# Sample states of the retention heads: values from float32 weights on four column groups, and their scores summed in the bank of the state products

## The chip, the cores and the metric

The kernel runs on one core of one Trainium2 chip. A core has five engines that run side by side and wait for each other by semaphores: PE (matrix products; the trace shows its weight loads apart, as PEld), DVE (vectors), ACT (activations and copies), POOL (general vector work, no access to the PE's accumulators) and SP, which here only issues transfers. Products go into PSUM, eight banks of 128 partitions x 512 float32. The metric is the device time of the whole kernel in microseconds (us). The kernel before takes 2159.27 us, the median of three runs (2158.21 to 2162.92); lower is better.

## The reference

The program is one inference step of one layer: 1024 prompt tokens, and 32 sample tokens (8 sequences of 4 tokens, each with its own past). Two branches read the same normalised input: retention (4 heads, keys of 256, values of 512) and latent attention. The change touches the retention of the sample tokens alone, which the reference computes with one chunk of four tokens for each sequence:

```python
def retention_chunk(q, k, v, s_prev, log_g):
    ...
    scores = jnp.einsum('bihd,bjhd->bhij', q, k) * dmask[None]
    intra = jnp.einsum('bhij,bjhe->bihe', scores, v)
    q_decay = jnp.exp((idx[:, None] + 1.0) * log_g[None, :])
    cross = jnp.einsum('bihd,bhde->bihe', q, s_prev) * q_decay[None, :, :, None]
    k_decay = jnp.exp((c - 1.0 - idx)[:, None] * log_g[None, :])
    s_new = (jnp.exp(c * log_g)[None, :, None, None] * s_prev
             + jnp.einsum('bjhd,bjhe->bhde', k * k_decay[None, :, :, None], v))
    return intra + cross, s_new
```

`q`, `k`, `v` are columns of `rmsnorm(x) @ w_in`, q and k turned by position. `intra + cross` is then group-normalised over each head's 512 values, scaled and multiplied by a SiLU gate. The states `s_prev` and `s_new` (8 x 4 x 256 x 512 float32, 16.8 MB each) are inputs and outputs of the kernel.

## The kernel before

**Stages.** The normalised input is kept turned (features on partitions, the 1056 = 1024 + 32 tokens along the free side) as eight pairs `xn[k]` of a rounded high part and the rest, in the fast float32 format (fp32r). A product of full accuracy is three fast ones, `mac` (L265 to L267): high by high, low by high, high by low. Stages follow each other: latents, page attention of the sample tokens, retention (the stage of the change, about 727 to 1340 us of the trace), latent attention of the prompt, and the output projections.

**A retention head.** `head_qk` (filler for the head before it) makes q and k of all tokens, 128 columns at a time, and leaves those of the sample tokens in `qS` and `kS`. `head_w` fetches the head's value weights, eight tiles of 128x512, and splits each into `X["W"][k]`, high and low. `prompt_chunks` then walks the eight prompt chunks. `values_of` makes a chunk's values in tiles tagged `vnh` and `vnl` (two buffers each). Behind the chunks comes `sample_state`.

**sample_state of before.** The sample tokens' values are made in eight steps of two fast products (L1006): the stationary side is `few`, 64 columns, the 32 sample columns of the high and the low input side by side; the moving side is the high and then the low split weight, 512 columns. Rows 0 to 31 and 32 to 63 of the result, copied out as `vs` (L1009), still have to be added; each later product that reads `vs` does so, because its other operand is repeated for both halves. L1012 makes the scores of the sample tokens, masked into `sm` (64x32). L1017 (`turn`) spreads the values to 128 rows, for row group r (32 rows) the tokens of sequences 2r and 2r + 1 in four copies, from which the update of the states takes a split of keys and values.

Then come four turns, one for each pair (i, m) of sequence parity and key half. A turn multiplies the queries with the states of four sequences at once (L1038): four products with a 128x32 stationary side, each on its own group of 32 columns of the array and so on its own 32 rows of the one bank `px`. Four products (L1045) make the update, DVE adds it to the states (L1047), and two transfers store them (L1049); the states of the turn after next come into the buffers that this frees (`states`, L978).

After the last turn the bank is copied out (L1054) as `xs`, and two float32 products close the head: the scores by the values (L1056), and `sel` by `xs` (L1057), which picks each token's row out of the four row groups. `group_norm` works on the 32 rows, and `gate_out` turns them with four transposes (L865) and multiplies them with the gate. For heads 0 to 2 `gate_out` is put off (`late`) into the next head's first chunk.

**What sets the order.** The functions are Python generators. A `yield` gives a cost, and `woven` lets that stream go on which is furthest behind, as a share of its declared total: the rest of a head's chunks and `sample_state` (27.9; 32.4 in the last head) against the next head's q, k and weights (50.3), in the last head against the remaining gate projections (31.8). What is woven in from there is the filler below. The order that the generators give is the priority for a planner, which sets each engine's order of instructions and the waits when the program is built, by its own model of times; a tile's slot is given on when the last reader of the old tile is done. On the chip each engine goes through its list in that order. All transfers here are issued by SP, so one that waits holds those behind it.

The last head differs: before the filler runs, five tiles of latents and two of rotary keys for the next stage are asked for (L1083, L1086), into the slots of the split value weights.

Of the kernel before, what the change touches and what calls it, by code (L numbers as in the profile page):

```python
# [9 lines left out]
F32 = mybir.dt.float32  # L10
F32R = mybir.dt.float32r
# [3 lines left out]
ALU = mybir.AluOpType  # L15
# [4 lines left out]
P = 128  # L20
D = 1024
SEQ = 1024
NB = 8
NS = 4
# [37 lines left out]
def _constants():  # L62
# [4 lines left out]
    def put(name, val, rows=P):  # L67
        o, w = at[name]
        c[:rows, o:o + w] = val
# [10 lines left out]
                                         for g in lg], 1), (4, 1)))  # L80
    put("sel", (p[:, None] % NR) == r[None, :])
    copy, token = p % 32 // 8, p // 32 * 8 + p % 8
# [8 lines left out]
    put("kd", np.exp((P - 1.0 - p[:, None]) * lg[None]) / 16)  # L91
    put("qdS", np.exp((rt[:, None] + 1.0) * lg[None]), NR)
    put("qd2S", np.exp(2 * (rt[:, None] + 1.0) * lg[None]), NR)
    put("kdS", (copy < 3)[:, None] * np.exp((NS - 1.0 - p[:, None] % NS) * lg[None]) / 16)
# [67 lines left out]
def decode_step(ctx: ExitStack, tc: tile.TileContext, A: dict, O: dict):  # L162
# [20 lines left out]
    def ac():  # L183
        return banks["pool"].tile([P, 512], F32, tag="ac", name="ac", bufs=3)
# [7 lines left out]
    def b32(ap):  # L192
        return ap.bitcast(F32)
# [576 lines left out]
    p4 = ph.enter_context(tc.tile_pool(name="p4", bufs=1))  # L770
    turn = p4.tile([2 * NR, P], F32, name="turn")
    sp.dma_start(turn, A["consts"][:2 * NR, at["turn"][0]:])
# [89 lines left out]
    def gate_out(h, on, n, cols, g):  # L862
        pt = tr()
        for f in range(4):
            pe.transpose(pt[:, f * P:f * P + n], on[:n, f * P:(f + 1) * P], ident[:n, :n])  # L865
# [116 lines left out]
    def sample_state(h, X):  # L982

        q, k = X["qS"], X["kS"]
        g4 = float(np.exp(NS * lg[h]))
        sl = slice(SEQ, NT)
        ks = p4.tile([P, 2, 4, 4, 8], F32, tag="knh", name="ks", bufs=2)
        for m in range(2):
# [5 lines left out]
        act.activation(kt, pt[:, :DK], AF.Copy, scale=C("kdS", h, 1))  # L994
        ks = p4.tile([P, 2, 2, NR], F32, tag="knh", name="ks2", bufs=2)
        for m in range(2):
            pool.tensor_copy(ks[:, m], k[:, m].unsqueeze(1).to_broadcast([P, 2, NR]))
        qm = p4.tile([P, 2, 288], F32, tag="row", name="qm", bufs=2)
        pool.memset(qm, 0.0)
        for m in range(2):  # L1000
            pool.tensor_copy(qm[:, m].rearrange("p (b x) -> p b x", x=36)[:, :, :NS], q[:, m].rearrange("p (b t) -> p b t", t=NS))
        yield 1.0
        ps = ac()
        for n in range(8):
            for part in range(2):
                pe.matmul(ps[:2 * NR], few[:, n, :], X["W"][n][part], start=n + part == 0, stop=n == 7 and part == 1)  # L1006
            yield 0.45
        vs = p4.tile([2 * NR, DV], F32, tag="vnl", name="vs", bufs=2)
        act.copy(vs, ps[:2 * NR])  # L1009
# [18 lines left out]
        yield 1.0  # L1028
        px = ac()
        g = gate_in(h, NR, sl)  # L1030
        out = O["ret_sample"][0].rearrange("(r i) h (m p) e -> i m h p r e", i=2, m=2)
        turns = [(i, m) for i in range(2) for m in range(2)]
        loaded = X["st"]
        for n, (i, m) in enumerate(turns):
            pairs = loaded.pop(0)
            st = [pairs[r // 2][:, r % 2, :] for r in range(4)]
            for r in range(4):
                ins = pe.matmul(px[32 * r:32 * r + 32, :], qm[:, m, 32 * (2 * r + i):32 * (2 * r + i) + 32], st[r],  # L1038
                                start=n == 0, stop=n == 3, tile_position=(0, 32 * r), skip_group_check=True)
                if n > 1:  # L1040
                    tc.keep_in_program_order(ins)
# [14 lines left out]
        pe.matmul(po[:NR], sm, vs, start=True, stop=False)  # L1056
        pe.matmul(po[:NR], C("sel"), xs, start=False, stop=True)  # L1057
# [558 lines left out]
```

## Time and profile before

| What | before |
|---|---|
| median of three runs | 2159.27 us |
| the profiled execution | 2150.59 us |
| span of its trace | 2148.7 us |
| PE busy | 2107.3 us, 98% |
| DVE, ACT, POOL busy | 1261.0, 723.7, 326.4 us |
| value steps L1006, all heads | 64 products, 18.6 us busy |
| state products L1038, all heads | 128 records, 18.9 us busy |
| granted PE clock, mean | 0.996 |

The profile is one execution. Each row of the trace is one instruction with its start from the beginning of the span and its length; equal ones in a row are merged with their count. An instruction's place is given by its line in the kernel (L1006), its result and operands by the names of tiles (`ac<-wv,few`: into a bank of tag ac, from `wv` and `few`), its form by the stationary side (128*64) and the moving side. Matmuls overlap: the next starts before the one before has ended, so lengths don't add up, but starts do. A float32 product shows as two records. A row of the list of waits reads: who waited, for whom, the sum, how many times, the longest.

### The profile page before, as it was taken

To read this page: it belongs to the slowest core of one execution; us is meant where nothing else is said; L and a number is where in the kernel's file an instruction comes from. 1 tells how busy PE (TensorE), PEld (TensorE's weight loads), DVE (VectorE), ACT (ScalarE), POOL (GpSimd) and SP (SyncE) were. 2 spreads that over 40 slices of the span, in tenths; PEclk is the share of its full clock that TensorE was granted. 3 is DMA by queue.
4 is the path that set the end of the run, shared out by engine and by line. 5 is a ranking of instruction groups with operands and counts; after the bars stand their busy time and mean duration, and the time that the engine had idled before them with its cause. 6 is when DMAs were issued, how large, how long until landed. Compare 5 with 4: busy or idle time off the path is not lost.

```text
span 2148.7 us, 38490 instructions
## 1 busy us (share of the span) xinstructions
PE 2107.3 (98%) x15192; PEld 1841.5 (86%) x15192; DVE 1261.0 (59%) x2832; ACT 723.7 (34%) x1514; POOL 326.4 (15%) x519
## 2 busy tenths in 40 slices
PE   8999999999999999999999999999999999999998
PEld 7898787777777998888888887788888999999998
DVE  5534556565565357676676764877776353444465
ACT  5412222342433322222222312454555341322343
POOL 2210111111110022222222220122211000000122
PEclk9999999999999999999999999999999999999999
DMA  7476656566564422644634637210112453324243
GB/s 209 124 221 232 233 194 234 212 231 237 200 231 165 124 65 72 206 115 121 197 75 147 179 87 259 58 45 18 38 51 80 151 176 95 100 80 127 79 144 118
DMA packets 325876, 307.83 MB, mean 143 GB/s; under 512 B 91648, under 2 KB 283264, under 8 KB 321600
## 3 DMA queue, kind: packets, MB, share of 16 engines
q1 hardware_dynamic: 316480, 221.50, 34.6%
q0 software_dynamic: 9216, 83.89, 10.5%
q8 instruction: 119, 1.95, 0.4%
q14 instruction: 61, 0.50, 0.1%
HBM read 236.96 MB, written 68.36 MB: 142 GB/s over the span
## 4 chain that ended last, share of the span: by engine, by line
PE 87%; DVE 2%; ACT 1%; DMA 1%; issue 1%; POOL 1%; SPq 0%; ACTq 0%; DVEq 0%; POOLq 0%
PE mm L265 22%; PE mm L266 20%; PE mm L267 20%; PE sc L655 4%; PE x L686 3%; PE ac L267 2%; PE ac L265 2%; PE ac L266 2%; PE mm L1313 2%; PE tr L1299 1%; PE tr L865 1%; PE ac L1038 1%; PE ac L1256 1%; PE x L680 1%; PE ac L887 1%
## 5 line engine op out<-in xcount | busy, mean ns | idle before, releaser
L265 PE MATMUL mm<-xh,wh 128*128 128x352 f32 x1344 | 455.2, 339 | 0.2
L267 PE MATMUL mm<-xh,wl 128*128 128x352 f32 x1344 | 434.3, 324 | 2.1 <-DVE wl L199 2.1
L266 PE MATMUL mm<-xl,wh 128*128 128x352 f32 x1344 | 434.9, 324 | 0.0
L265 PEld LDWEIGHTS mm<-xh,wh 128*128 128x128 f32 x1344 | 252.2, 188 | 90.5 <-issue 76.5
L266 PEld LDWEIGHTS mm<-xl,wh 128*128 128x128 f32 x1344 | 253.3, 188 | 3.3 <-issue 1.0
L267 PEld LDWEIGHTS mm<-xh,wl 128*128 128x128 f32 x1344 | 253.0, 188 | 3.3 <-DVE wl L199 2.6
L199 DVE TENSOR_TENSOR wl<-wr,wh 128x512 fp32r<-128x512 f32 (+2 forms) x251 | 173.8, 704 | 120.4 <-ACT wh L246 101.8
L246 ACT CAST wh<-wr 128x512 fp32r<-128x512 f32 x216 | 129.8, 618 | 294.9 <-PE mm L266 221.0
L651 DVE STREAM_TRANSPOSE kt<-craw 128x512 f32<-128x512 f32 x256 | 160.7, 681 | 84.8 <-PE sc L655 79.7
L416 ACT ACTIVATE gev<-mm 128x352 f32<-128x352 f32 x120 | 55.6, 464 | 237.2 <-PE mm L267 157.0
L267 PE MATMUL mm<-gh,wl 128*128 128x352 f32 x384 | 124.3, 324 | 0.0
L267 PE MATMUL mm<-mh,wl 128*128 128x352 f32 x384 | 124.3, 324 | 0.0
L265 PE MATMUL mm<-mh,wh 128*128 128x352 f32 x384 | 124.3, 324 | 0.0
L265 PE MATMUL mm<-gh,wh 128*128 128x352 f32 x384 | 124.3, 324 | 0.0
L266 PE MATMUL mm<-ml,wh 128*128 128x352 f32 x384 | 124.2, 324 | 0.0
L266 PE MATMUL mm<-gl,wh 128*128 128x352 f32 x384 | 124.2, 323 | 0.0
L265 PE MATMUL mm<-wv,xh 128*128 128x512 f32 x256 | 103.7, 405 | 0.0
L266 PE MATMUL mm<-wv,xh 128*128 128x512 f32 x256 | 100.9, 394 | 0.0
L267 PE MATMUL mm<-wv,xl 128*128 128x512 f32 x256 | 100.7, 394 | 0.0
L655 PE MATMUL sc<-kt,q 32*32 32x512 f32 x2560 | 91.2, 600 | 0.0
L854 ACT ACTIVATE on<-ac,gb,gs 128x512 f32<-128x512 f32 (+1 forms) x36 | 28.0, 778 | 179.6 <-DVE gb L852 179.6
L1546 POOL TENSOR_TENSOR xr<-x1h,x1l 128x352 f32<-128x352 f32 x24 | 27.1, 1154 | 389.9 <-DVE pT L199 311.9
(382 smaller groups left out, 4540.0 us busy)
## 6 DMA issues: line engine op xcount, KB each, us to landing
wr<-in_w_in_dram SPq DMA_DIRECT2D x144, 256.0 KB, 3.1
st<-in_state_ret_dram SPq DMA_DIRECT2D x32, 512.0 KB, 4.5
out_ret_sample_dram<-st SPq DMA_DIRECT2D x32, 512.0 KB, 3.8
wr<-in_w_ple_gate_dram SPq DMA_DIRECT2D x48, 256.0 KB, 2.9
gt<-gev SPq DMA_DIRECT2D x48, 176.0 KB, 3.9
gl<-go SPq DMA_DIRECT2D x16, 528.0 KB, 5.8
gate<-ga SPq DMA_DIRECT2D x16, 528.0 KB, 3.5
g<-gt SPq DMA_DIRECT2D x32, 256.0 KB, 3.2
```

The source lines that it names most:

```text
L199: dve.tensor_tensor(out=out, in0=src, in1=b32(hi), op=ALU.subtract)
L246: hi_by[0](hi, raw)
L265: pe.matmul(out, wh, xh, start=first, stop=False)
L266: pe.matmul(out, wh, xl, start=False, stop=False)
L267: pe.matmul(out, wl, xh, start=False, stop=last)
L416: act.activation(t, ps, func)
L651: dve.transpose(kt[:, 2 * i + s].rearrange("p (n r) -> p n r", r=32), src)
L655: pe.matmul(sc[32 * v:32 * v + 32, q, :], Q["q4"][qs_, j + v // 2, 2 * (g % 2) + v % 2, :], kt[qs_, v, :], start=n == 0, stop=n == NJ // 2 ...
L686: pe.matmul(pv[32 * v:32 * v + 32, :KL], pT[:, n, 32 * v:32 * v + 32], keys[v % 2][:, 8 * (v // 2) + n, :], start=n == 0, stop=n == 7, til ...
L854: act.activation(on[:n], po, AF.Identity, bias=nb[:n], scale=s[:n])
L1313: pe.matmul(po[:, :256], v[a][w], t[:, x, 256 * a:256 * a + 256], start=j + a + part == 0, stop=False, skip_group_check=True)
L1546: pool.tensor_tensor(out=xr, in0=b32(x1[f][0][:, sl]), in1=b32(x1[f][1][:, sl]), op=ALU.add)
```

## The change

- The values of the sample tokens come from the plain float32 weights, read from memory once more: eight tiles `wvS` of 128x512 (256 KB) a head, in the slots of `vnh` and `vnl`. Four are asked for at the start of `sample_state`, each of the other four after the value step whose slot it takes.
- The stationary side is `xS`, the sum of the high and low input (128x32, float32). A step is four float32 products, one for each 128 of the 512 columns and each on its own group of 32 columns of the array, into 32 rows and 128 columns of the bank.
- Four copies put these blocks on the diagonal of `vs`, now 128x512, made once, with zeros elsewhere. `turn` has 128 rows and adds the row groups.
- The scores are made for 128 rows and masked into `sm`, 128x128, with zeros outside the eight rows of each group. Their product with `vs` opens the bank `px`, and the state products add to it.
- The copy of the bank and the two closing products are gone. `group_norm` works on the 128 rows of the bank, and `gate_out` turns and picks the rows in one, by float32 products with `sel` (four of 128x128 by 128x32) in place of the transposes.
- Yields: 2.5 instead of 1.0 ahead of the values; 0.24 instead of 0.45 for a value step, 1.0 for the fourth; 0.3 instead of 1.0 at the end.

The constants `sel`, `qdS` and `qd2S` follow the new rows. The rest of the diff:

```diff
-    few = p4.tile([P, 8, 2 * NR], F32R, name="few")
+    xS = p4.tile([P, 8, NR], F32, name="xS")
     for k in range(8):
-        for part in range(2):
-            pool.tensor_copy(few[:, k, part * NR:(part + 1) * NR], b32(xn[k][part][:, SEQ:]))
+        pool.tensor_tensor(out=xS[:, k], in0=b32(xn[k][0][:, SEQ:]), in1=b32(xn[k][1][:, SEQ:]), op=ALU.add)
+    vs = p4.tile([P, DV], F32, name="vs")
+    pool.memset(vs, 0.0)
...
-            pe.transpose(pt[:, f * P:f * P + n], on[:n, f * P:(f + 1) * P], ident[:n, :n])
+            o = pt[:, f * P:f * P + n]
+            if n == P:
+                pe.transpose(o, on[:, f * P:(f + 1) * P], ident)
+            else:
+                pe.matmul(o, on[:, f * P:(f + 1) * P], C("sel"), start=True, stop=True)
...
+        def weights(k):
+            raw = p4.tile([P, DV], F32, tag="vn" + "hl"[k % 2], name="wvS", bufs=2)
+            sp.dma_start(raw, w_in[k * P:(k + 1) * P, C_RV + h * DV:C_RV + (h + 1) * DV])
+            return raw
+
+        raws_ = [weights(k) for k in range(4)]
...
-        yield 1.0
+        yield 2.5
         ps = ac()
         for n in range(8):
-            for part in range(2):
-                pe.matmul(ps[:2 * NR], few[:, n, :], X["W"][n][part], start=n + part == 0, stop=n == 7 and part == 1)
-            yield 0.45
-        vs = p4.tile([2 * NR, DV], F32, tag="vnl", name="vs", bufs=2)
-        act.copy(vs, ps[:2 * NR])
+            for r in range(4):
+                pe.matmul(ps[r * NR:(r + 1) * NR, :P], xS[:, n], raws_[n][:, r * P:(r + 1) * P], start=n == 0, stop=n == 7,
+                          tile_position=(0, r * NR), skip_group_check=True)
+            if n < 4:
+                raws_.append(weights(n + 4))
+            yield 1.0 if n == 3 else 0.24
+        for r in range(4):
+            rs = slice(r * NR, (r + 1) * NR)
+            act.copy(vs[rs, r * P:(r + 1) * P], ps[rs, :P])
         pss = tr()
         for m in range(2):
-            pe.matmul(pss[:2 * NR, :NR], ks[:, m].rearrange("p c x -> p (c x)"), q[:, m], start=m == 0, stop=m == 1)
-        sm = p4.tile([2 * NR, NR], F32, tag="sms", name="sms", bufs=1)
-        dve.tensor_tensor(out=sm, in0=pss[:2 * NR, :NR], in1=C("maskS", h, NR, 2 * NR), op=ALU.mult)
+            pe.matmul(pss[:, :NR], ks[:, m].rearrange("p c x -> p (c x)"), q[:, m], start=m == 0, stop=m == 1)
+        sm = p4.tile([P, 4, NR], F32, tag="smr", name="sms", bufs=1)
+        pool.memset(sm, 0.0)
+        dve.tensor_tensor(out=sm[:, :, :8], in0=pss[:, :NR].rearrange("p (r x) -> p r x", x=8),
+                          in1=C("maskS", h, NR).rearrange("p (r x) -> p r x", x=8), op=ALU.mult)
...
         px = ac()
+        pe.matmul(px, sm.rearrange("p r x -> p (r x)"), vs, start=True, stop=False, skip_group_check=True)
...
-                                start=n == 0, stop=n == 3, tile_position=(0, 32 * r), skip_group_check=True)
+                ins = pe.matmul(px[32 * r:32 * r + 32, :], qm[:, m, r, i], st[r], start=False, stop=n == 3,
+                                tile_position=(0, 32 * r), skip_group_check=True)
...
-        xs = p4.tile([P, DV], F32, tag="row", name="xsb", bufs=2)
-        act.copy(xs, px)
-        po = ac()
-        pe.matmul(po[:NR], sm, vs, start=True, stop=False)
-        pe.matmul(po[:NR], C("sel"), xs, start=False, stop=True)
-        on = group_norm(po[:NR], NR, C("qdS", h, 1, NR), C("qd2S", h, 1, NR))
-        yield 1.0
+        on = group_norm(px, P, C("qdS", h, 1), C("qd2S", h, 1))
+        yield 0.3
```

More of the change, by code (lines that the diff above doesn't have):

```diff
@@ L80, in _constants @@
                                          for g in lg], 1), (4, 1)))
-    put("sel", (p[:, None] % NR) == r[None, :])
+    put("sel", (p[:, None] // 32 * 8 + p[:, None] % 32 == r[None, :]) & (p[:, None] % 32 < 8))
     copy, token = p % 32 // 8, p // 32 * 8 + p % 8
@@ L91, in _constants @@
     put("kd", np.exp((P - 1.0 - p[:, None]) * lg[None]) / 16)
-    put("qdS", np.exp((rt[:, None] + 1.0) * lg[None]), NR)
-    put("qd2S", np.exp(2 * (rt[:, None] + 1.0) * lg[None]), NR)
+    put("qdS", np.exp((t[:, None] + 1.0) * lg[None]))
+    put("qd2S", np.exp(2 * (t[:, None] + 1.0) * lg[None]))
     put("kdS", (copy < 3)[:, None] * np.exp((NS - 1.0 - p[:, None] % NS) * lg[None]) / 16)
@@ L770, in decode_step @@
     p4 = ph.enter_context(tc.tile_pool(name="p4", bufs=1))
-    turn = p4.tile([2 * NR, P], F32, name="turn")
-    sp.dma_start(turn, A["consts"][:2 * NR, at["turn"][0]:])
-    few = p4.tile([P, 8, 2 * NR], F32R, name="few")
+    turn = p4.tile([P, P], F32, name="turn")
+    sp.dma_start(turn, A["consts"][:, at["turn"][0]:])
+    xS = p4.tile([P, 8, NR], F32, name="xS")
     for k in range(8):
-        for part in range(2):
-            pool.tensor_copy(few[:, k, part * NR:(part + 1) * NR], b32(xn[k][part][:, SEQ:]))
+        pool.tensor_tensor(out=xS[:, k], in0=b32(xn[k][0][:, SEQ:]), in1=b32(xn[k][1][:, SEQ:]), op=ALU.add)
+    vs = p4.tile([P, DV], F32, name="vs")
+    pool.memset(vs, 0.0)
     tok = slots(p4, "tok", 4)
@@ L994, in sample_state @@
         act.activation(kt, pt[:, :DK], AF.Copy, scale=C("kdS", h, 1))
-        ks = p4.tile([P, 2, 2, NR], F32, tag="knh", name="ks2", bufs=2)
+        ks = p4.tile([P, 2, 4, NR], F32, tag="knh", name="ks2", bufs=2)
         for m in range(2):
-            pool.tensor_copy(ks[:, m], k[:, m].unsqueeze(1).to_broadcast([P, 2, NR]))
-        qm = p4.tile([P, 2, 288], F32, tag="row", name="qm", bufs=2)
+            pool.tensor_copy(ks[:, m], k[:, m].unsqueeze(1).to_broadcast([P, 4, NR]))
+        qm = p4.tile([P, 2, 4, 2, 32], F32, tag="row", name="qm", bufs=2)
@@ L999, in sample_state @@
         pool.memset(qm, 0.0)
         for m in range(2):
-            pool.tensor_copy(qm[:, m].rearrange("p (b x) -> p b x", x=36)[:, :, :NS], q[:, m].rearrange("p (b t) -> p b t", t=NS))
-        yield 1.0
+            for i in range(2):
+                pool.tensor_copy(qm[:, m, :, i, NS * i:NS * i + NS], q[:, m].rearrange("p (r i t) -> p r i t", i=2, t=NS)[:, :, i])
+        yield 2.5
         ps = ac()
         for n in range(8):
-            for part in range(2):
-                pe.matmul(ps[:2 * NR], few[:, n, :], X["W"][n][part], start=n + part == 0, stop=n == 7 and part == 1)
-            yield 0.45
```

1 line of the change is left out of this document (removed).

## The prediction

> **What bounds the kernel now.** I read the page's busy shares first, then who made the PE wait in the retention stage that the change touches (860 to 1345 us), then the PE's instructions in order of time there, and last the DMA share and the queue around the last head.
>
> ```profile
> PE 2107.3 (98%) x15192; PEld 1841.5 (86%) x15192; DVE 1261.0 (59%) x2832; ACT 723.7 (34%) x1514; POOL 326.4 (15%) x519
> ...
> PE ac L265 <- POOL wqr L196: 1.7, 1, 1.7
> PE ac L267 <- DVE ll L199: 0.9, 1, 0.9
> PE ac L1038 <- DMA st<-in_state_ret_dram: 0.5, 1, 0.5
> ```
>
> The last three rows are the PE's longest waits in those 485 us, 3.1 us together, each of them once, and all in or behind the last head; the first two belong to the next stage. The reader sees that the sample states of the first three heads run with the PE never idle to speak of: there a PE microsecond saved is one saved, and work of ACT, DVE, POOL or DMA costs nothing until the PE waits for it. So the sum is one of PE time, made against the profiled execution (2150.59 us) and then carried to the median of 2159.27 us by the same difference; the 8.7 us between these two aren't explained by anything here.
>
> **The old pieces, priced.** Head 0, the PE's starts in order of time (start, length, instruction):
>
> ```profile
> 874.20 0.63 PE L1006 MATMUL ac<-wv,few 128*64 128x512 f32 x2
> 874.67 0.32 PE L265 MATMUL mm<-xh,wh 128*128 128x352 f32 x1
> ...
> 879.45 2.01 PE L1006 MATMUL ac<-wv,few 128*64 128x512 f32 x8
> ...
> 884.67 1.12 PE L1017 MATMUL tr<-vs,turn 64*128 64x512 f32 x2
> 885.72 0.43 PE L265 MATMUL mm<-xh,wh 128*128 128x352 f32 x1
> ...
> 889.31 1.06 PE L1038 MATMUL ac<-st,qm 128*32 128x512 f32 x8
> 890.30 0.50 PE L1045 MATMUL ac<-vst,kx 32*128 32x512 f32 x2
> ...
> 920.84 0.32 PE L267 MATMUL mm<-xh,wl 128*128 128x352 f32 x1
> 921.09 1.04 PE L1056 MATMUL ac<-vs,sms 64*32 64x512 f32 x2
> 922.06 1.05 PE L1057 MATMUL ac<-xsb,cst 128*32 128x512 f32 x2
> 923.03 0.43 PE L265 MATMUL mm<-xh,wh 128*128 128x352 f32 x1
> 923.30 0.32 PE L266 MATMUL mm<-xl,wh 128*128 128x352 f32 x1
> 923.46 0.32 PE L267 MATMUL mm<-xh,wl 128*128 128x352 f32 x1
> ```
>
> Starts, not lengths, give what a matmul costs the PE. A filler matmul (352 columns) is followed after 0.16 us (923.30 to 923.46). A value step of old, two products of 512 columns, takes 874.67 - 874.20 = 0.47 us, and the filler behind it has its usual length of 0.32 (behind a float32 product 0.43): eight steps, **3.76 us a head**. A float32 product shows as two records, and it has edges: the filler ahead of it holds 0.25 instead of 0.16 (920.84 to 921.09, +0.09), and the first filler behind it 0.27 (923.03 to 923.30, +0.11). The two products that closed a head (scores by values, and the sum over row groups) thus cost (923.30 - 0.16) - (920.84 + 0.16) = **2.14 us a head**.
>
> **What the new value step costs.** Two rows have its form, a 128x32 stationary on each of four column groups: L1038 above with 512 columns, and the page attention's L686 with 256, eight steps in a row:
>
> ```profile
> 218.03 3.66 PE L686 MATMUL x<-craw,pT 128*32 128x256 f32 x64
> 221.62 0.43 PE L265 MATMUL mm<-xh,wh 128*128 128x352 f32 x1
> ```
>
> L1038 takes 0.99 us for two passes of 512 columns with the four groups side by side; L686 takes 3.59 us for sixteen passes of 256, as much as eight of 512. Fixed part plus passes: f + 2p = 0.99 and f + 8p = 3.59 give p = 0.43 and f = 0.12 us. A pass of 128 columns is a quarter of p, so a step is 2 x 0.108 = 0.22 us, and each uninterrupted burst of steps adds its edges, 0.09 + 0.12 + 0.11 = 0.32 us. A lone step costs 0.54 us, dearer than the old 0.47; steps in a row cost half of it. **So everything hangs on how many bursts the eight steps form.** By the yields, a step advances its stream by 0.24 of 27.9 and one filler group of three matmuls advances the other by 0.441 of 50.3, 0.0086 against 0.0088: they alternate, but for an occasional weight-staging yield without PE work. I take 6.5 bursts for heads 0 to 2: 8 x 0.22 + 6.5 x 0.32 = 3.8 us, no gain. In the last head the filler's share is 0.441 of 31.8 against 0.24 of 32.4, so about two steps go with a group: 4.5 bursts, 3.2 us, a gain of 0.6. Bounds for each head: 4 and 8 bursts, 3.0 and 4.3 us, hence -3.0 to +2.2 us over four heads; I take **-0.5**.
>
> The Trainium skill, page "TensorE: Matmul & The Clock Gate", section "Back-to-back issue gap", speaks against such narrow products: in a stream of load-and-matmul pairs it gives about 81 ns a pair at 128 columns. By that the eight records of a step would take an estimated 0.65 us instead of 0.22, and 32 steps 13.8 us more; the L686 row, where 64 pairs took 3.59 us, 56 ns each at twice the columns, does not agree, so this goes among the rivals with a small chance.
>
> **The rest of the PE's sum.**
>
> ```profile
> 171.81 1.87 PE L552 MATMUL mm<-early 128*128 128x32 f32 x16
> 173.51 0.41 PE L265 MATMUL mm<-xh,wh 128*128 128x352 f32 x1
> ...
> 933.34 0.43 PE L865 MATMUL tr<-cst,on 32*128 32x32 f32 x4
> 933.70 0.71 PE L887 MATMUL ac<-q,k 128*128 128x128 f32 x4
> ```
>
> - Closing products removed: 4 x -2.14 = -8.6 us.
> - Scores by values, now the opening product of the state bank: a 128x512 float32 product like L1017, 885.72 - 884.67 = 1.05 us, 4 x 1.05 = +4.2. It stands straight ahead of the state products, whose entry edge is already paid; if filler comes between, another 0.2 each, +0.8 at most.
> - The sample rows' turn before the gate: four transposes (933.70 - 933.34 = 0.36 us) become four float32 products with 32 moving columns, eight records of L552's kind, (173.51 - 171.81) / 16 = 0.106 us each, 0.85: 4 x 0.49 = +2.0.
> - The score product makes 128 rows instead of 64. Its four records have 32 moving columns like L552's and can at most come to 0.106 each, 0.42 us; the growth lies between 0 and that, I take 0.12: 4 x 0.12 = +0.5.
>
> Sum with the value steps: -8.6 + 4.2 + 2.0 + 0.5 - 0.5 = **-2.4 us** (bounds -5.4 and +2.3).
>
> **Off the PE.**
>
> ```profile
> L1009 ACT COPY vs<-ac x4: 576/580/582, 881.5 to 1300.6; 64x512 f32<-64x512 f32 x4
> ...
> L818 ACT COPY qS<-q x8: 218/219/221, 766.3 to 1183.7; 128x32 f32<-128x32 f32 x8
> ```
>
> ACT copies the values out once now (0.58 us) and four times 128 columns after the change, each between the two rows: 0.9 to 2.3 us. In head 0 the copy ends at 882.1 and the product that reads it starts at 884.67; those 2.6 us of filler are the cover, so it costs 0, and without it 0.3 to 1.7 us a head. The copy of the state bank goes away. POOL gains a memset and some copies, at 15% of its time; DVE's group norm covers 128 rows instead of 32, over the same 512 columns. The split value weights lose their last reader: their slots come free after the last chunk's values instead of after the value steps, so the next head's weights, and in the last head the next stage's latents, can come into them earlier.
>
> **The new transfers and their wait.** Per head eight tiles of 256 KB. The first four wait for the last two chunks' value buffers; each of the others waits until a value step has read the slot that it takes, and it stands on SP, which is in order: behind it wait next weights, gate stores and state transfers.
>
> ```profile
> wr<-in_w_in_dram SPq DMA_DIRECT2D x144, 256.0 KB, 3.1
> lat<-latD SPq DMA_DIRECT2D x5, 512.0 KB, 5.1
> ...
> 1290.00:1295.00 5.00, 5.00 (x32) 4.54 (x32) 3.42 (x9) 1.70 (x3) 0.74 (x5) 1.00 0.92 337
> ```
>
> The last row is five microseconds of the last head, its last two columns DMA share and GB/s. From step 0 to step 4 lie four steps and yields of 3 x 0.24 + 1.0 = 1.72, which stand for 3.1 us of filler in heads 0 to 2: about 5.2 us. A tile of this size lands in 3.1 us by the median of 144: no stall, cost 0; in the 5.1 us of a latent it would just arrive. In the last head the filler is 1.7 us, so the step lead is 3.5 us, the DMA engines are 0.92 busy, and the first tiles come behind 3.1 MB (five latents of 512 KB and two rotary keys of 256), which now start at the same moment. Bounds there: 0 (latents moved ahead into the freer time) and 4 us (first tiles 2 us late, second four another 2); I take **+1.5**.
>
> **The end of the last head.**
>
> ```profile
> ACT krA L1109 <- DMA go<-g: 2.9, 1, 2.9
> ...
> 1339.11 0.32 PE L267 MATMUL mm<-xh,wl 128*128 128x352 f32 x1
> 1341.13 0.36 PE L265 MATMUL ac<-wqr,lh 128*128 128x256 f32 x1 [1.70 <-POOL wqr L196]
> ```
>
> The filler, not the chain of states, ends last (1339.11), and then the PE waits 1.7 and 0.9 us for the next stage's splits. The group norm no longer waits for the closing products, which stood behind 3.8 of filler yield and took 1.9 us more (921.09 to 923.03 in head 0); estimated from both it starts 4 us earlier, and the gated store with it, so the rotary keys' splits (krA), which wait for that store and now crowd ACT and DVE at this point, can run before. Bounds 0 (the splits wait for the filler's inputs to come free) and -2.6 (both waits gone); I take **-0.7**.
>
> Total -2.4 + 1.5 - 0.7 = -1.6 us: 2149.0 for the profiled execution, **2157.7 us** against the median of 2159.27. A measurement here tells 0.2%, 4.3 us, from no change; this is inside it.
>
> **Rivals.**
> - *Late tiles in every head* (slower). The second four tiles land later than the filler covers, because each is issued only after its step and SP holds it behind other waits. It decides where issue and landing together pass 5.2 us. At a landing of 6.5 us and 0.4 for the issue: 1.7 us in three heads, 3.4 in the last, and 2 for its first tiles, 10.5 instead of the 1.5 taken: 2166.7 us. For: SP is in order, and the last head's DMA share is 0.92. Against: 3.1 us for this very size. Chance 0.15.
> - *Bursts run together* (faster). If the planner, which sees the tiles arrive in groups, puts the steps in two bursts a head, they cost 8 x 0.22 + 0.64 = 2.4 us: 4 x -1.36 = -5.4 instead of -0.5, and with the end's full -2.6: 2157.7 - 4.9 - 1.9 = 2150.9 us. For: the four old steps that ran together in heads 0 to 2. Against: the yields. Chance 0.2.
> - *The four groups do not run side by side at 128 columns* (the change does not do what it says). Serial, a step is eight passes of 0.108 = 0.86 us instead of 0.22: 32 x 0.64 = +20.5, 2178 us; at half of that overlap, 2168. Against: both rows of this form. Chance 0.05.
>
> **How the numbers follow.** The forecast case has 0.6. Its bounds add up to 2151.3 and 2165.6; all at one end is unlikely, and its own range is 2153 to 2162, with 0.05 of its chance faster by over 0.2% and 0.02 slower. Of the bursts' 0.2, 0.18 lies beyond 0.2%; of the late tiles' 0.15, 0.12; of the serial groups' 0.05, 0.04. Faster: 0.05 + 0.18 = 0.23. Slower: 0.02 + 0.12 + 0.04 = 0.18. Same: 0.59. The range 2151 to 2167 takes in the faster rival and the slower one to its price, and leaves out the serial groups.
>
> **What would show it.** Right: a value step of 0.5 to 0.6 us where it stands alone and 0.22 more for each in a burst; six or seven bursts in heads 0 to 2; no product after the last state product; the gate turn at 0.85 us; PE waits on the new tiles near zero in heads 0 to 2 and some 1 to 2 us in the last. Wrong: value steps at 0.8 us or more, or PE waits on the new tiles of over 1 us in each head (slower); steps in two bursts and no waits of the next stage (faster); any change of the PE's order outside this stage by more than 2 us, which I count at nothing.

## The result and the profile after

The changed kernel takes 2166.83 us (median of 19 runs, 2162.39 to 2171.88) against 2159.73 for the kernel before beside it. The ratio is **1.0031**, 95% interval 1.0025 to 1.0037: slower by about 7 us. Forecast were 2157.7 us and no measurable change. So the time lies in the range, and the sign is wrong. It also lies beside the 2166.7 of the rival with late tiles, and that is luck: of the 10.5 us that the rival gave to the tiles, they cost 3.1.

One execution can't be set against another over its whole span: in the twelve profiled kernels the retention's first score product stands anywhere between 784.0 and 796.2 us, although the PE's instructions ahead of it are the same, in the same order. They form two groups: 784 to 789 us in the kernel before and in kernels 5 to 10 below, 793 to 796 in the changed one and in kernels 1 to 4, where the PE waits some 5 us for ACT and DVE between 300 and 727 us, and not at all in the first group. Beside kernels 5 to 10 the kernel before has medians of 2153.0 and 2153.6 us, beside kernels 1 to 4 and the changed one 2159.9 and 2159.7, and 2150.59 us, the time of its profiled execution, is among the runs beside kernels 5 to 8. So the 8.7 us that the prediction left open are most likely a difference between chips, ahead of the stage of the change; why one chip waits there stays open. I therefore compare the retention stage by itself, from the first score product of its first head to the first prompt scores of the next stage. For the kernel before, and then for the changed one, the PE's instructions in order of time have these as first and last:

```profile
785.15 0.61 PE L887 MATMUL ac<-q,k 128*128 128x128 f32 x4
...
1366.37 0.45 PE L1256 MATMUL ac<-k,q 128*128 128x448 f32 x1
```

```profile
793.03 0.61 PE L892 MATMUL ac<-q,k 128*128 128x128 f32 x4
...
1380.64 0.45 PE L1271 MATMUL ac<-k,q 128*128 128x448 f32 x1
```

That is 581.2 us before and 587.6 after: **+6.4**, which agrees with the runs, although the two executions are most likely of different chips, and what lies behind it differs by 0.5 us. By heads, from one head's first score product to the next one's, it is +0.4, +1.1, +0.5 and, for the last head, +4.3. The busy shares don't tell this (98% on PE both times). The PE's longest waits in the stage do (total, times, longest):

```profile
PE ac L1019 <- DMA wvS<-in_w_in_dram: 3.1, 5, 0.8
PE ac L1065 <- DVE vst L1039: 2.4, 3, 0.8
PE ac L265 <- POOL wqr L196: 1.4, 1, 1.4
...
PE ac L267 <- DVE ll L199: 0.8, 1, 0.8
```

Two rows are new, 5.5 us together: value steps (L1019) waiting for weight tiles, and state updates (L1065) waiting for the DVE's row `vst`. All eight waits lie in heads 0 to 2. Smaller rows grew with them: all of the PE's waits in these three heads together are 7.9 us, against 1.3 before. Here is head 0 of the changed kernel (start, length, instruction, in brackets the idle time and who ended it):

```profile
885.11 0.32 PE L267 MATMUL mm<-xh,wl 128*128 128x352 f32 x1
885.36 0.43 PE L1019 MATMUL ac<-wvS,xS 128*32 128x128 f32 x8
885.72 0.43 PE L265 MATMUL mm<-xh,wh 128*128 128x352 f32 x1
885.98 0.32 PE L266 MATMUL mm<-xl,wh 128*128 128x352 f32 x1
886.14 0.32 PE L267 MATMUL mm<-xh,wl 128*128 128x352 f32 x1
886.40 0.86 PE L1019 MATMUL ac<-wvS,xS 128*32 128x128 f32 x24
887.19 0.43 PE L265 MATMUL mm<-xh,wh 128*128 128x352 f32 x1
887.46 0.33 PE L266 MATMUL mm<-xl,wh 128*128 128x352 f32 x1
...
889.95 0.42 PE L1019 MATMUL ac<-wvS,xS 128*32 128x128 f32 x8 [0.56 <-DMA wvS<-in_w_in_dram]
...
896.94 0.33 PE L267 MATMUL mm<-xh,wl 128*128 128x352 f32 x1
897.11 1.02 PE L1036 MATMUL tr<-vs,turn 128*128 128x512 f32 x2
897.56 0.72 PE L265 MATMUL mm<-xh,wh 128*128 128x352 f32 x1
898.12 0.32 PE L266 MATMUL mm<-xl,wh 128*128 128x352 f32 x1
...
898.93 1.02 PE L1049 MATMUL ac<-vs,sms 128*128 128x512 f32 x2
...
901.76 0.50 PE L1065 MATMUL ac<-vst,kx 32*128 32x512 f32 x2 [0.81 <-DVE vst L1039]
```

The price of a piece is the time from the filler ahead of it to the second filler behind it, less two fillers of 0.16. A lone value step takes 885.98 - 885.11 - 0.32 = 0.55 us, three in a row 887.46 - 886.14 - 0.32 = 1.00. My model said 0.54 and 0.98. **These pieces cost what was forecast; the waits are what was not.** Six bursts were formed, five lone steps and one of three.

Where the second four requests of head 0 stand on SP, behind two gate loads (SP in order of time):

```profile
882.93 2.88 SPq L860 DMA_DIRECT2D g<-gt  x2
885.91 2.26 SPq L995 DMA_DIRECT2D wvS<-in_w_in_dram  x4
```

Step 4 wanted its tile at 889.95 - 0.56 = 889.39, only 3.5 us after the first of these requests started, and got it 4.0 us after. How long such tiles take in general this trace can't tell: it has the landings of 3 of the 32. Kernel 5, whose PE has the same order in heads 0 to 2, has all of them:

```profile
DMA to landing us min/median/max: 2.9/4.1/5.3
```

Who was late with `vst`: the turn was done at 898.13, but the DVE's order has a weight split ahead of the first reading of it, begun 0.5 us later, and a product of q between its two passes (DVE in order of time, changed kernel):

```profile
898.59 1.42 DVE L199 TENSOR_TENSOR wv<-wr,wv 128x512 fp32r<-128x512 f32 x1
899.93 0.68 DVE L1038 CAST vr<-tr 128x512 fp32r<-128x512 f32 x1
900.54 0.51 DVE L804 TENSOR_TENSOR q<-q,cosR 128x352 f32<-128x352 f32 x1
900.97 0.73 DVE L1039 SCALAR_TENSOR_TENSOR vst<-vr,cst,tr 128x512 fp32r<-128x512 f32 x1
```

The same two rows before:

```profile
885.83 0.69 DVE L1019 CAST vr<-tr 128x512 fp32r<-128x512 f32 x1 [0.19 <-PE tr L1017]
...
887.04 0.74 DVE L1020 SCALAR_TENSOR_TENSOR vst<-vr,cst,tr 128x512 fp32r<-128x512 f32 x1
```

Before, `vst` was done at 887.78 and read at 890.30, 2.5 us to spare: 21 filler matmuls stood between the turn and the state products. After the change 6 stand there, and the opening product, and the DVE begins 1.8 us after the turn's end instead of at once. The whole order is made ahead of time by a planner that simulates the engines, and with the new pieces it weaves the two streams differently: 1.0 of yield bought 21 matmuls before and 6 now.

**The last head** has no wait on a tile, and loses most. Its way to the next stage's first product is 4.4 us longer (137.2 us against 132.8 from the head's start), although the PE waits less on it (2.1 us against 2.5) and the filler is the same: it loses by PE work. SP before, and SP of the changed kernel:

```profile
1294.72 6.24 SPq L1083 DMA_DIRECT2D lat<-latD  x5
```

```profile
1286.74 0.33 SPq L1098 DMA_DIRECT2D lat<-latD  x1
...
1306.18 7.05 SPq L995 DMA_DIRECT2D wvS<-in_w_in_dram  x5
```

From the head's start (1208.34 and 1218.31) the latents are requested at 68 us instead of 86, and the value weights come behind them, at 88. The planner puts the value steps late: without the transfers (kernel 3 below) the first stands at 87.6 us from the head's start, here at 94.1, against 85.0 before, and the turn at 103.8 against 94.2. What is late next is the state turns, with too little filler left to separate them in a regular way:

```profile
1324.01 1.06 PE L1058 MATMUL ac<-st,qm 128*32 128x512 f32 x8
1325.00 0.50 PE L1065 MATMUL ac<-vst,kx 32*128 32x512 f32 x2
...
1335.03 1.05 PE L1058 MATMUL ac<-st,qm 128*32 128x512 f32 x4
1336.01 0.43 PE L267 MATMUL mm<-xh,wl 128*128 128x352 f32 x1
1336.37 0.50 PE L1065 MATMUL tr<-vst,kx 32*128 32x512 f32 x1
1336.80 0.43 PE L265 MATMUL mm<-xh,wh 128*128 128x352 f32 x1
```

A state product over four groups takes 0.99 us (1324.01 to 1325.00). Over two it takes 0.98 (1335.03 to 1336.01): half the work at the whole price. A single update (one record) costs 0.43, as much as four side by side. Two of the four turns are broken up like this. Before, one was, and only in its state products, the last, where a wait for a state's transfer parts them:

```profile
1322.42 1.05 PE L1038 MATMUL ac<-st,qm 128*32 128x512 f32 x4
1324.02 1.05 PE L1038 MATMUL ac<-st,qm 128*32 128x512 f32 x4 [0.55 <-DMA st<-in_state_ret_dram]
```

### The profile page after: what moved, and what is told of

Same layout as the page of the kernel before. It is cut to its first block, busy times and chain, and to the rows that moved or that the text cites. A ratio compares the mean times of both kernels' runs of the same rounds, so it can differ in the third digit from the quotient of the medians.

```text
span 2162.5 us, 38971 instructions
## 1 busy us (share of the span) xinstructions
PE 2112.3 (98%) x15392; PEld 1841.7 (85%) x15392; DVE 1257.4 (58%) x2832; ACT 720.4 (33%) x1522; POOL 333.3 (15%) x524
## 4 chain that ended last, share of the span: by engine, by line
PE 60%; DVE 4%; issue 4%; ACT 1%; POOL 1%; DMA 1%; DVEq 0%; ACTq 0%; POOLq 0%; SPq 0%
PE mm L265 15%; PE mm L267 14%; PE mm L266 14%; PE ac L266 2%; PE ac L267 2%; PE ac L265 2%; PE mm L1328 2%; PE tr L1314 1%; PE ac L1271 1%; PE sc L655 1%; PE x L686 1%; PE ac L1272 1%; PE ac L1274 1%; PE ac L1275 1%; PE ac L1273 1%
## 5 line engine op out<-in xcount | busy, mean ns | idle before, releaser
L265 PEld LDWEIGHTS mm<-xh,wh 128*128 128x128 f32 x1344 | 252.2, 188 | 87.9 <-issue 77.5
L855 ACT ACTIVATE on<-ac,gb,gs 128x512 f32<-128x512 f32 x36 | 28.1, 780 | 150.1 <-DVE gb L853 149.7
```

Source lines behind the costliest of these rows:

```text
L265: pe.matmul(out, wh, xh, start=first, stop=False)
L855: act.activation(on[:n], po, AF.Identity, bias=nb[:n], scale=s[:n])
```

## The experiments

My **theory 1** after the result: the products are cheaper, as forecast, and the loss is made by when things run. It has three places: tiles late in heads 0 to 2 (3.1 us), the row `vst` late (2.4), and the last head's order (some 4 us). **Theory 2**, in two forms: the loss sits in the work itself, either in the float32 steps with their edges or in the scores' half.

All stages below are in us, from the PE's starts as above, heads as differences from before; ratios are to the kernel before on the same chip, with the interval. Kernels 1 to 4, 5 to 8 and 9 and 10 ran on three different chips, where the kernel before has medians of 2159.9, 2153.0 and 2153.6.

| kernel | ratio (95%) | stage | heads 0, 1, 2, last |
|---|---|---|---|
| before | 1 | 581.2 | |
| changed | 1.0031 (1.0025 to 1.0037) | 587.6 | +0.4, +1.1, +0.5, +4.3 |
| 1 values' half | 1.0080 (1.0066 to 1.0094) | 593.7 | +1.8, +1.8, +1.7, +7.2 |
| 2 scores' half | 1.0003 (0.9994 to 1.0012) | 580.9 | -1.0, +1.1, -0.8, +0.2 |
| 3 no transfers | 1.0005 (0.9996 to 1.0014) | 584.0 | +0.5, +1.4, +0.5, +0.5 |
| 4 longer yield | 1.0016 (1.0007 to 1.0025) | 587.1 | -0.3, +0.1, +0.5, +5.5 |
| 5 late latents | 1.0016 (1.0004 to 1.0027) | 584.5 | +0.2, +0.9, +1.6, +0.6 |
| 6 both of these | 1.0005 (0.9996 to 1.0014) | 579.0 | +0.7, -0.7, -0.9, -1.4 |
| 7 old values, last head | 0.9998 (0.9989 to 1.0007) | 580.4 | -0.2, +0.1, -0.3, -0.5 |
| 8 scores, transposes | 0.9978 (0.9968 to 0.9987) | 577.1 | -1.1, -0.6, -1.4, -1.0 |
| 9 two bursts | 0.9971 (0.9961 to 0.9982) | 579.0 | -3.0, -2.5, -2.7, +5.9 |
| 10 all in order | 0.9949 (0.9937 to 0.9961) | 571.5 | -2.6, -2.9, -3.6, -0.7 |

The stage of the one profiled execution and the runs agree within 5 us; a difference below that rests on the interval of the runs. Kernels 4, 6 and 7 have the same order of the PE's work in heads 0 to 2, and one head of theirs differs by up to 1.4 us between them: a smaller difference of a single head shows nothing. The rows before and 5 to 10 were profiled in the first group of above, the others in the second.

**1. The values' half alone.** Value steps and added transfers as changed; closing products and gate as before, the scores too, but for the 128 rows that `vs` has now.

> Only the values' half of the change: float32 value steps on four column groups from weights read again; the scores, the closing products and the four gate transposes are those of the kernel before. Theory 1 (late tiles, and an order of the PE's work that their arrival sets: the PE waits 3.1 us for weight tiles and 2.4 us for the states' row in three heads, and in the last head value steps that come late break the state turns in halves, some 4 us): all of these come with this half, against about 0.9 us a head that the steps themselves save, so 4 to 7 us slower than before, ratio 1.002 to 1.003, with PE waits of 4 us or more on the new tiles and the states' row. Theory 2 (the loss sits in the scores' half: the opening product and the turn by a product of the rows cost more than the closing products did): within 2 us of before or faster, ratio 0.999 to 1.001.

Slower than the whole change: 1.0080. The waits in the stage:

```profile
PE ac L1014 <- DMA wvS<-in_w_in_dram: 3.7, 5, 1.1
PE ac L1057 <- DVE vst L1032: 3.5, 3, 1.2
```

The sign is theory 1's, the size is not: I expected 4 to 7 us; the stage gives +12.5, the runs 17. The waits are 1.7 us longer than in the changed kernel, the closing products stay, and the last head is broken up more (+7.2). The loss is in this half, and the scores' half hid part of it.

**2. The scores' half alone.** Value steps from the split weights, nothing read again; the scores open the state bank.

> Only the scores' half: the score product opens the state bank, no closing products, four float32 products turn the gate's rows; the value steps are the old ones, from the split weights, and nothing is read again. Theory 1: the PE's starts of the changed kernel give -2.04 for the closing products, +0.95 for the opening one, +0.45 for the turn and about +0.1 for the scores, so -0.5 us a head, 2 us in all faster than before, ratio 0.999, and no PE wait over 1 us on the states' row or on a transfer. Theory 2: this half carries the loss, 4 to 7 us slower, ratio 1.002 to 1.003.

Ratio 1.0003, no change. It does not carry the loss, so that form of theory 2 falls. The gain of 2 us that I expected did not show either; one row has it:

```profile
PE tr L867 <- ACT on L854: 2.1, 4, 1.0
```

The PE waits for group norms of the prompt's chunks ahead of their transposes (0.8 us before). Ahead of the norm of the longest of these waits ACT itself waited 1.1 us, for the DVE; why just there, no run separates.

**3. No added transfers.** One line:

```
         def weights(k):
-            raw = p4.tile([P, DV], F32, tag="vn" + "hl"[k % 2], name="wvS", bufs=2)
-            sp.dma_start(raw, w_in[k * P:(k + 1) * P, ...])
-            return raw
+            return b32(X["W"][k][0])
```

The steps read the high part of the split weights instead; the low part is left out.

> The changed kernel without its added transfers: the value steps read the high part of the split weights that the values of the prompt use, as float32. [...] Every product of the changed kernel is there. Theory 1: without late tiles the PE's sum shows, some 1.4 us a head less than before; with the wait on the states' row still there (up to 0.8 us in a head) ratio 0.997 to 1.000, at least 6 us below the changed kernel. Theory 2 (the float32 steps with their edges cost more than the split ones, whatever feeds them): ratio 1.002 or more.

Ratio 1.0005, 5.6 us below the changed kernel by the ratios' difference of 0.0026 (3.6 by the stage): the second form of theory 2 falls as well, though the kernel stands just above what theory 1 gave (0.997 to 1.000). With no tile to wait for, the planner ran seven steps together (56 records between fillers) and put the turn directly behind their copy, and new waits opened:

```profile
PE mm L267 <- DVE wl L199: 4.5, 3, 1.5
PE tr L1034 <- ACT vs L1024: 1.9, 3, 0.6
```

Waits of 6.4 us, against 0.2 in these two places before, ate the gain. That the work is cheaper the prices of the pieces show, not this run; the order decides whether it is seen.

**4. More filler behind the turn.** `yield 1.0` between the turn and the state products becomes `yield 2.0`; 18 filler matmuls stand there now.

> The changed kernel with one number changed: 2.0 instead of 1.0 is yielded between the product that turns the values and the state products, so 12 more filler matmuls stand there. Theory 1: the PE's wait of 0.8 us on the states' row goes in each of the first three heads, 2.4 us faster than the changed kernel, ratio to before 1.002. Rival: the twelve matmuls are taken from other places of the stream, and an equal wait opens there, or the last head's plan shifts: no change against the changed kernel, ratio 1.003.

The row of L1065 on `vst` is gone, heads 0 to 2 fall from +2.1 to +0.3 together, the ratio to 1.0016, 3.2 us by the ratios against 2.4 expected. The stage as a whole gains only 0.5, since the last head stands at +5.5. The tiles are still late:

```profile
PE ac L1019 <- DMA wvS<-in_w_in_dram: 4.0, 5, 0.9
```

**5. Latents later in the last head.** The requests for latents and rotary keys move behind the value steps in the program.

> The changed kernel, but in the last head the latents and rotary keys of the next stage (five transfers of 512 KB and two of 256) are requested behind the value steps instead of ahead of the weight tiles. Theory 1 (in the last head the tiles come behind these transfers, so the value steps start 11 us late and the state turns are broken in halves): the value steps start about 10 us earlier, and of the last head's 4.3 us over the kernel before, 2 or more are won back: ratio to before 1.001 to 1.002. Rival (the last head loses by the float32 steps' own work, or the later latents are missed by the next stage instead): ratio 1.003 or more, with a PE wait on the latents' splits.

The last head falls from +4.3 to +0.6, the ratio to 1.0016. It did not happen quite as I wrote it: the planner left four of the five latents where they were (68 to 73 us behind the head's start) and moved only the last one and the rotary keys, from 75 to 77 us to 93 to 94. That was enough: the first weight tile is requested 79.5 us in, not 87.9, the first step runs at 87.9, not 94.1. That is 6 us, not 10. The last two turns stay broken, one of them with no filler in between. What the start of the tiles waited for in the changed kernel, the queue or the planner's reckoning of the transfers, I can't tell apart. The rival, that later latents would be missed, shows no more of a PE wait on their splits than 1.0 us, against 0.9 before.

**6. Both edits.**

> Both edits at once: the latents behind the value steps of the last head, and 2.0 instead of 1.0 yielded between the turn of the values and the state products. Nothing of the change is undone, only when its neighbours run. Theory 1 (the loss is the order of the work, in two places): heads 0 to 2 within 0.5 us of before together, as with the longer yield alone, and the last head within 2 us, ratio 1.000 to 1.001. Rival (something of the added transfers or of the steps costs PE time wherever they stand): ratio 1.002 or more.

Ratio 1.0005, no change; the stage is 2.2 us below before. Nothing of the change is undone here, so the loss of 7 us was the order in these two places. The PE still waits for tiles, 3.7 us in five places, the longest 2.1, and the cheaper work pays for that.

**7. Old value steps in the last head alone** (with the yield of 4).

> The changed kernel with the 2.0 of yield behind the turn, and in the last head alone the value steps of the kernel before (two split products a step, from weights that are there already, no added transfers); the scores' half stays in all four heads. Theory 1: heads 0 to 2 as with the longer yield alone (+0.3 us over before together), the last head as where only the scores' half was made (+0.2 us): ratio 1.000, at least 4 us below the changed kernel. Rival (the last head's loss is the scores' half, as its gate turn and norm now end the stage): the last head stays 3 us or more above before, ratio 1.002.

Ratio 0.9998, the last head at -0.5: the scores' half costs nothing there, and the rival falls. With 3, 5 and 6 this puts the last head's loss on its late value weights.

**8. The scores' half with plain transposes.** The gate's rows turned by four transposes of 128 rows, eight of each 32 columns read (against kernel 2, cut):

```
-                pe.matmul(o, on[:, f * P:(f + 1) * P], C("sel"), start=True, stop=True)
+            pe.transpose(pt[:, f * P:(f + 1) * P], on[:, f * P:(f + 1) * P], ident)
...
-        yield 0.3
+        yield 1.0
```

> The scores' half alone, with two edits: the gate's rows are turned by four plain transposes of 128 rows (as the prompt's are), of which the eight wanted columns of each 32 are read, instead of four float32 products; and 1.0 instead of 0.3 is yielded behind the group norm. From rows: a 128x128 transpose takes 0.11 us against 0.21 for the product, 0.4 us a head, 1.6 in all; the wait of 1.0 us on ACT in the second head of the scores' half should go with the yield. Expected: 1 to 2.5 us under the kernel before, ratio 0.999. Rival (the turn is hidden, or the wait moves): ratio 1.000 to 1.001.

0.9978, 4.7 us faster than before by the runs and 4.1 by the stage, twice what I expected; the waits on ACT fell from 2.1 to 0.6 us in the stage. Four transposes cost 0.44 us where the four products cost 0.88.

**9. Value steps in two bursts**, in the changed kernel:

```
-        yield 2.5
+        yield 3.0
...
-            yield 1.0 if n == 3 else 0.24
+            yield 4.0 if n == 3 else 1.0 if n == 7 else 0
```

> The changed kernel with other yields around the value steps alone: nothing between the steps of each half, so that four stand together, 39 filler matmuls (6.3 us) between the halves and 12 more ahead of the turn. Theory 1 with my price of a value step (0.22 us, and 0.32 for the edges of each burst): heads 0 to 2 save four bursts, 4 x 0.32 = 1.3 us each, and most of the wait on the second four tiles, which landed 5.2 us by the median behind their issue; the states' row is waited for less. Heads 0 to 2 together 1 to 3 us below before instead of 2.1 above, the last head as in the changed kernel (+4): ratio 1.000 to 1.001. Rival (the edges are no price of a burst, and the tiles are late however long the gap): ratio 1.003 as in the changed kernel.

0.9971. Heads 0 to 2 are at -8.1 us together, where I expected -1 to -3: my expectation left the removed waits (5.5 us) almost out and took four bursts' edges for the gain. The last head is as bad as ever (+5.9).

**10. All of it:** 9's yields, 4's, 5's latents, 8's transposes.

> All edits together: value steps in two bursts with 6.3 us of filler between, 12 filler matmuls ahead of the turn and 18 behind it, latents behind the value steps in the last head, and the gate's rows turned by four plain transposes. Every product of the change but the gate's is there, and all its transfers. Theory 1: heads 0 to 2 at -2.14 for the closing products, +0.95 for the opening one, -0.6 for the turn, -1.6 to -1.3 for the value steps, +0.1 for the gate, so about -2.8 us each, the last head -1.5 to -2.5: 8 to 11 us under the kernel before, ratio 0.995 to 0.996, and below the scores' half with transposes (0.998). Rival (the tiles stay late and the rest of the queue with them, so that the values' half gives nothing even so): ratio 0.998.

**0.9949: 11 us faster than before** and some 18 faster than the changed kernel by the two ratios, with every added transfer in place. Kernel 8, the scores' half with the same transposes, gave 4.7; by the difference, an estimate across two chips, the values' half is worth some 6 once its order is right. The waits of the stage, and a burst in head 0:

```profile
PE ac L265 <- ACT lh L1142: 2.4, 1, 2.4
PE tr L866 <- ACT on L855: 1.2, 2, 0.8
...
PE ac L1027 <- DMA wvS<-in_w_in_dram: 0.9, 1, 0.9
```

```profile
880.49 0.32 PE L267 MATMUL mm<-xh,wl 128*128 128x352 f32 x1
880.74 1.08 PE L1027 MATMUL ac<-wvS,xS 128*32 128x128 f32 x32
881.75 0.43 PE L265 MATMUL mm<-xh,wh 128*128 128x352 f32 x1
882.01 0.32 PE L266 MATMUL mm<-xl,wh 128*128 128x352 f32 x1
...
888.25 1.08 PE L1027 MATMUL ac<-wvS,xS 128*32 128x128 f32 x32
```

Four steps take 882.01 - 880.49 - 0.32 = 1.20 us, and 4 x 0.22 + 0.32 is 1.20. The halves stand 888.25 - 880.74 = 7.5 us apart, more than the longest landing here (5.3), and the one wait for a tile that is left is in the last head. The longest wait, 2.4 us, is at the next stage's first products, where the kernel before waits 1.7 and 0.9. The first three heads make 9.1 of the stage's 9.8 us.

## Why the prediction was wrong, point by point

- **The value steps' price** held: 0.55 us alone, 1.00 for three, 1.20 for four, against 0.54, 0.98 and 1.20. Six bursts in heads 0 to 2 (6.5 taken), eight in the last (4.5 taken): there each step stood apart, about 3.5 x 0.32 = 1.1 us. Without the transfers (kernel 3) the last head forms six, so the tiles explain two of these bursts and no more.
- **The Trainium skill**, page "TensorE: Matmul & The Clock Gate", section "Back-to-back issue gap": by its 81 ns a pair, a burst of four steps (32 records) would take an estimated 2.6 us. It took 1.20. The groups do run side by side at 128 columns, and the trace does not agree with that figure for this form; the rival with 0.05 falls.
- **Closing, opening, gate turn**: -2.14, +0.95 and +0.45 a head, against -2.14, +1.05 and +0.49. Right.
- **Scores**: forecast +0.12, in heads 0 to 2 they got 0.4 us cheaper. Before, the four records stood in two pairs, one straight behind the last four value steps (at 881.40; 881.89 - 879.29 - 0.32 - 4 x 0.47 = 0.40) and one between fillers (at 882.15; 882.64 - 881.89 - 0.32 = 0.43); now they stand together, 895.33 - 894.55 - 0.32 = 0.46.
- **The turn of the values** was counted at nothing, and the row was in the prediction: it now has 128 rows instead of 64 and costs 0.86 us (898.12 - 896.94 - 0.32) instead of 1.25, measured the same way in the kernel before. A gain of 0.4 a head that I missed.
- **So the work of heads 0 to 2 fell by about 1.5 us each** (-2.14 + 0.95 + 0.45 - 0.39 - 0.37, the value steps unchanged at 3.75), three times what the sum said (0.5). The waits in these heads rose from 1.3 to 7.9 us, 2.2 a head. That makes +0.7, as measured.
- **First failed step: "no stall, cost 0" for the tiles in heads 0 to 2.** I set 5.2 us of lead against 3.1 of landing. In head 0 the lead was 889.39 - 885.36 = 4.0, since three steps fell into one burst and took their filler out of it; the request came 0.55 behind step 0 and the tile 4.0 behind the request, which makes the wait of 0.56. By the median of kernel 5 a tile takes 4.1. The second four are requested together, where the 144 that I took the 3.1 from are requested singly or in pairs. 3.1 us in five waits. My rival of late tiles had the place right and the price too high (1.7 a head, measured 1.0), and I gave it 0.15.
- **Second failed step: the cover of the turn.** I named the cover of the copy ahead of the turn (ACT) and not the one behind it (DVE's two passes to `vst`). It had 2.5 us to spare, lost 15 filler matmuls (2.4 us) for an opening product of 0.95, and the DVE came to it 1.8 us late, with a weight split ahead in its order. Waits of 2.4 us.
- **Third failed step: the last head, +1.5 for tiles and -0.7 at the end.** No tile was waited for there; I had the lateness right (the latents crowd ahead) and not its form. The planner put the value steps later, and the turns that broke behind them made the PE's work up to the next stage 4.9 us longer (4.4 of time and 0.5 less of waits), more than the 4 us that were my bound for the tiles. The next stage's waits went from 1.7 + 0.9 to 1.4 + 0.8, -0.4 of the -0.7, and waits of 0.8 and 0.6 on weight splits came in behind them, where there was one of 0.2.
- **"Bursts run together"** (2150.9 us) was named as a rival with the right price for a step. It did not come about by itself; put there by yields it paid even more in heads 0 to 2 (kernel 9), since it gave the tiles their lead as well; the last head kept eight lone steps.

The sum took the filler around the pieces, and with it every cover, from the plan of the kernel before, and gave no reason for it: I spoke of a changed order only outside the stage, where indeed nothing moved (0.5 us behind it). That the order inside the stage stays is the assumption that fell. Whenever one piece changes, the planner weaves everything anew, and kernels 2 and 3 opened waits at the prompt's transposes and at the weight splits, which neither of them touches.

## What to carry to other kernels

Where the bottleneck engine is kept busy by filler between the pieces of a chain, list for every producer and consumer how much filler stands between them, and what of it stays when the pieces change: two such covers lost here (2.4 and 3.1 us) and a few small waits outweighed work that had become 4.5 us cheaper in three heads. A planned order must be read from the plan that the change makes, not from the one that it replaces. When a change of this kind loses, move the neighbours first: three yields, a few requests and a cheaper turn took the same change from +7 to -11 us.

## What the runs showed of the hardware that was not expected

- A float32 product of 512 columns with a stationary side of 128 columns is dearer with 64 rows than with 128. The turn, before:

```profile
884.26 0.48 PE L267 MATMUL mm<-xh,wl 128*128 128x352 f32 x2
884.67 1.12 PE L1017 MATMUL tr<-vs,turn 64*128 64x512 f32 x2
...
885.99 0.32 PE L266 MATMUL mm<-xl,wh 128*128 128x352 f32 x1
```

  The second filler of the first row starts at 884.42, so it costs 885.99 - 884.42 - 0.32 = 1.25 us, against 0.86 with 128 rows. The opening product repeats it: 1.05 with 64 rows (kernels 2 and 8), 0.95 with 128. With 32 stationary columns there is no such difference: the closing products took 0.97 with 64 rows and 0.97 with 128 (921.09, 922.06, 923.03 in the prediction's lines). Why, no run here shows.
- Column groups and row groups left empty save nothing: two state products 0.98 us against 0.99 for four, one update 0.43 against 0.43 for four.
- In kernels 5, 6, 9 and 10, whose traces have every landing, the added 256 KB tiles took 4.1 to 4.2 us by the median, the 144 weight tiles of the same size and the same traces 3.5 to 3.6, and 3.1 in the kernel before. About half of the added tiles are asked for in packs of four, the others singly or in pairs. No run separates the pack from what else was in flight.
